# A batched matmul of 64x64 matrices: each load issued one store earlier in the DMA queue

## Chip, cores and metric

The kernel runs on one core of a Trainium2 chip. The metric is the device time of one execution in microseconds (us); lower is better.

## Reference

```python
def setup_inputs():
    return {
        "a": np.random.randn(1024, 64, 64).astype(np.float32),
        "b": np.random.randn(1024, 64, 64).astype(np.float32),
    }

def reference(a, b):
    return np.matmul(a, b).astype(np.float32)
```

There are 1024 independent products of two 64x64 matrices. Each of a, b and the output has 16.78 MB in float32.

## The kernel before

The 1024 matrices are cut in eight groups of 128 (`s` = 0 to 7, `n_s` = 8) for the loads, and in sixteen groups of 64 (`t` = 0 to 15, `n_t` = 16) for products and stores; group s feeds t = 2s and t = 2s + 1.

**Loads.** `load_a(s)` (line 79) and `load_pair(s)` (line 109) each issue four DMAs from POOL (GpSimd), of 32 partitions each. Each reads 512 KiB of float32 and writes 256 KB of bf16. "Tile a s" is what `load_a(s)` fills, "b pair s" what `load_pair(s)` fills. The first a tile is loaded otherwise, in float32 by four DMAs of the SP and ScalarE queues, into two buffers of the output pool (`load_first_a`). The pools `a_pool` and `b_pool` have three buffers each, so tile a s takes the buffer of a s-3 (a 1, 2 and 3 take the first three), and a load waits until VectorE has read what the buffer held.

**Turning.** VectorE transposes 32x32 blocks of a (`turn_a`, line 129) and b (`turn`, line 121), two instructions for each group s. `spread` (lines 142 and 149) copies the turned a of one t into a block diagonal tile `at_bd`, three quarters on VectorE and one on ScalarE; near both ends each engine does half. There are three such tiles (`N_BD`).

**Products and evacuation.** `multiply(t)` runs TensorE's matmuls (line 195) into PSUM, and ScalarE copies the results to an output tile `o_sb` (line 213, eight copies for each t). t = 14 is accumulated in another order, and t = 15 is cut in four parts whose copies ScalarE and VectorE share. Eight output tiles rotate.

**Stores.** `multiply` only notes a tile's stores in `held`; `store(t)` issues them. Each t has two halves of 512 KiB, both issued from POOL (line 222); only the last tile has four parts of 256 KiB on the SP and ScalarE queues.

**Order.** Each engine runs its instructions in the order in which the program writes them. Ahead of the loop come the first loads of a and b, groups 0 to 2. In the loop over t the order is `multiply(t)`, then the turns and spreads of later tiles, then `store(t)`. The table `BESIDE` (line 37) names the load that goes out with each store: half of its DMAs behind the first half of the store, half behind the second.

```python
        for i, piece in enumerate(held.pop(t)):
            piece()
            if load:
                load(s, range(2 * i, 2 * i + 2))
```

So POOL's queue of DMAs is: half store, two loads, half store, two loads, and so on, from store 0 to store 9; stores 10 to 14 have no loads beside them.

Of the kernel before, what the change touches and what calls it, by code (L numbers as in the profile page):

```python
# [12 lines left out]
def kernel(  # L13
# [21 lines left out]
    B_AHEAD = 3  # L35
    N_BD = 3
    BESIDE = {
        0: ("a", 3),
        1: ("p", 3),
        2: ("a", 4),  # L40
        3: ("p", 4),
        4: ("a", 5),
        5: ("p", 5),
        6: ("a", 6),
        7: ("p", 6),
        8: ("a", 7),
        9: ("p", 7),
    }
    LAST_QUEUE = {0: nc.sync, 2: nc.sync, 4: nc.scalar, 6: nc.sync}

# [28 lines left out]
    def load_a(s, hs=range(4)):  # L79
        if s not in a_tiles:  # L80
            a_tiles[s] = a_pool.tile([128, 4096], bf16, name="a_sb")
        for h in hs:
            nc.gpsimd.dma_start(out=a_tiles[s][32 * h : 32 * h + 32], in_=ap_v[s, h])  # L83

    def load_first_a():

        raw = [
            o_pool.tile([128, 8, 4, 64], fp32, name="o_sb")[:].rearrange(
                "p gh w n -> p (gh w n)"
            )  # L90
            for _ in range(2)
        ]
        parts = [raw[h % 2][:, 1024 * (h // 2) : 1024 * (h // 2) + 1024] for h in range(4)]
        for h in range(4):
            (nc.scalar if h % 2 else nc.sync).dma_start(out=parts[h], in_=a_v[0, h])
        a_tiles[0] = parts

    def turn_first_a(h):
        if h == 0:
            a_tiles["first"] = first.tile([128, 4, 1024], bf16, name="a_bf")  # L100
            at_tiles[0] = work.tile([128, 4, 8, 4, 4, 4], fp32, name="at_sb")
        rows = a_tiles["first"][:, h]
        (nc.scalar.copy if h else nc.vector.tensor_copy)(rows, a_tiles[0][h])  # L103
        nc.vector.transpose(  # L104
            at_tiles[0][:, h].rearrange("p g w mp vo -> p w vo g mp"),
            rows.bitcast(fp32).rearrange("p (vo w kp) -> p w vo kp", vo=4, w=4),
        )

    def load_pair(s, hs=range(4)):
        if 0 in hs:  # L110
            b_tiles[s] = b_pool.tile([128, 4096], bf16, name="b_sb")
        for h in hs:
            nc.gpsimd.dma_start(out=b_tiles[s][32 * h : 32 * h + 32], in_=bp_v[s, h])  # L113

    def turn(s, u):
        if u == 0:
            bbf_tiles[s] = work.tile([128, 32, 128], bf16, name="b_bf")
        rows = b_tiles[s][:].bitcast(fp32).rearrange("p (kp u np) -> p u np kp", kp=32, u=2)
        cols = bbf_tiles[s][:].rearrange("p g c -> p (g c)").bitcast(fp32)
        cols = cols.rearrange("p (g u np) -> p u np g", g=32, u=2)  # L120
        nc.vector.transpose(cols[:, u], rows[:, u])  # L121

    def turn_a(s, half):
        if half == 0:
            at_tiles[s] = work.tile([128, 32, 4, 4, 4], fp32, name="at_sb")
        rows = a_tiles[s][:].bitcast(fp32)
        rows = rows.rearrange("p (mp vo w kp) -> p mp vo w kp", mp=4, vo=4, w=4)
        cols = at_tiles[s][:].rearrange("p g w mp vo -> p mp vo w g")
        nc.vector.transpose(  # L129
            cols[:, 2 * half : 2 * half + 2].rearrange("p mp vo w g -> p (mp vo) w g"),  # L130
            rows[:, 2 * half : 2 * half + 2].rearrange("p mp vo w kp -> p (mp vo) w kp"),
        )
# [21 lines left out]
    def spread_all(t):  # L154
        on_act = (2, 3) if t < 2 or t >= n_t - 2 else (3,)
        spread(t, [h for h in range(4) if h not in on_act], nc.vector.tensor_copy)
        spread(t, on_act, nc.scalar.copy)

    def store(t):
        kind, s = BESIDE.get(t, ("", 0))  # L160
        load = {"a": load_a, "p": load_pair}.get(kind)
# [4 lines that stand above are left out]
# [52 lines left out]
    def multiply(t):  # L218
        o_sb = o_pool.tile([128, 8, 4, 64], fp32, name="o_sb")

        def put(lo, n):
            store_queue(t, lo).dma_start(  # L222
                out=o_v[t, :, lo : lo + n, :],
                in_=o_sb[:, lo : lo + n].rearrange("p gh w n -> p (gh w n)"),
            )

        act, dve = nc.scalar.copy, nc.vector.tensor_copy
        if t == n_t - 2:
            halves = [o_psum.tile([128, 4, 4, 64], fp32, name="o_ps") for _ in range(2)]
            for u in range(2):  # L230
                for half in range(2):
                    products(t, 8 * half, 8, halves[half], (u,))
                    if u == 1:
                        evacuate(t, 8 * half, 8, halves[half], o_sb, act)
        elif t == n_t - 1:
            for g0 in range(0, 16, 4):
                o_ps = t_psum.tile([128, 2, 4, 64], fp32, name="t_ps")
                products(t, g0, 4, o_ps)
                evacuate(t, g0, 4, o_ps, o_sb, dve if g0 % 8 else act)
        else:  # L240
            for g0 in (0, 8):
                o_ps = o_psum.tile([128, 4, 4, 64], fp32, name="o_ps")
                products(t, g0, 8, o_ps)
                evacuate(t, g0, 8, o_ps, o_sb, act)
        n = 2 if t == n_t - 1 else 4
        held[t] = [lambda lo=lo: put(lo, n) for lo in range(0, 8, n)]

    with tc.manual_schedule():
        load_first_a()
        nc.vector.memset(warm[:, 0:1], 0.0)  # L250
        nc.scalar.copy(warm[:, 1:2], warm[:, 0:1])  # L251
        nc.vector.memset(bd_tiles[0][:], 0.0)  # L252
        nc.gpsimd.memset(bd_tiles[1][:], 0.0)  # L253
        load_pair(0)
        load_a(1)
        load_pair(1)
        nc.gpsimd.memset(bd_tiles[2][:], 0.0)  # L257
        load_a(2)
        load_pair(2)
        for h in range(4):  # L260
            turn_first_a(h)
        spread_all(0)
        turn(0, 0)
        turn(0, 1)
        spread_all(1)
        turn_a(1, 0)
        turn_a(1, 1)
        spread_all(2)
        turn(1, 0)
        turn(1, 1)  # L270
        for t in range(n_t):
            s, half = t // 2, t % 2
            multiply(t)
            if t == 1:
                spread_all(3)
            elif half == 0 and s + 1 < n_s and t:
                turn_a(s + 1, 0)
                turn_a(s + 1, 1)
                spread_all(t + 2)
            elif half and s + 1 < n_s:  # L280
                if s + 1 == n_s - 1:
                    spread_all(t + 2)
                turn(s + 1, 0)
                turn(s + 1, 1)
                if s + 1 < n_s - 1:
                    spread_all(t + 2)
            store(t)
# [30 lines left out]
```

## Time and profile before

| What | Value |
|---|---|
| Median of 3 runs | 128.21 us (127.74 to 128.29) |
| Profiled execution | 128.62 us, of which its span is 126.8 us |
| Busy in the span | VectorE 102.9, ScalarE 96.0, POOL 64.9, TensorE 54.9 us |
| HBM | 33.55 MB read, 16.78 MB written, 397 GB/s over the span |
| POOL's DMA queue (q0) | 31.46 MB landed, 91.9% of the 16 DMA engines' span |
| Mean granted TensorE clock | 0.682 |

A page of the profile cuts the span in 40 slices of 3.17 us; a digit is the busy share of a slice in tenths. In a timeline, a row has its start, its length, the engine, the source line, the operation and, in brackets, the idle time before it with what ended it. In the windows, a row has the stretch, its length, the busy time of TensorE, its weight loads, VectorE, ScalarE and POOL with the instructions in parentheses, the granted clock, the DMA share and GB/s. The GB/s are those of what the DMAs wrote, so a load that turns float32 into bf16 counts half of what it reads. An issue row's length is POOL's time for writing the DMA's descriptors, not the transfer.

### The profile page before, as it was taken

To read this page: it belongs to the slowest core of one execution; us is meant where nothing else is said; L and a number is where in the kernel's file an instruction comes from. 1 tells how busy PE (TensorE), PEld (TensorE's weight loads), DVE (VectorE), ACT (ScalarE), POOL (GpSimd) and SP (SyncE) were. 2 spreads that over 40 slices of the span, in tenths; PEclk is the share of its full clock that TensorE was granted. 3 is DMA by queue.
4 is the path that set the end of the run, shared out by engine and by line. 5 is a ranking of instruction groups with operands and counts; after the bars stand their busy time and mean duration, and the time that the engine had idled before them with its cause. 6 is when DMAs were issued, how large, how long until landed. Compare 5 with 4: busy or idle time off the path is not lost.

```text
span 126.8 us, 2680 instructions
## 1 busy us (share of the span) xinstructions
PE 54.9 (43%) x1088; PEld 51.7 (41%) x1088; DVE 102.9 (81%) x93; ACT 96.0 (76%) x151; POOL 64.9 (51%) x96
## 2 busy tenths in 40 slices
PE   0000019028645485847352942047510777079400
PEld 0000019028645484847352932046510776079300
DVE  4956999999999999999969696896949789780810
ACT  2157920399999999999999889918898299999700
POOL 8962797428544655625544446474554464333100
PEclk9999999955586555555955599657755555555965
DMA  2999999999999999999999999999999999999992
GB/s 59 392 327 209 212 217 217 212 215 207 264 293 257 264 290 292 291 292 278 265 275 290 291 288 284 275 275 275 296 288 283 275 273 279 383 406 396 343 342 99
DMA packets 8875, 34.76 MB, mean 274 GB/s; under 512 B 1568, under 2 KB 2592, under 8 KB 6944
## 3 DMA queue, kind: packets, MB, share of 16 engines
q0 software_dynamic: 7200, 31.46, 91.9%
q1 hardware_dynamic: 1104, 1.84, 4.3%
q10 hardware_dynamic: 560, 1.31, 2.7%
q8 instruction: 8, 0.13, 0.4%
q14 instruction: 3, 0.02, 0.0%
HBM read 33.55 MB, written 16.78 MB: 397 GB/s over the span
## 4 chain that ended last, share of the span: by engine, by line
DMA 57%; DVE 15%; ACT 7%; issue 7%; PE 5%; POOL 3%; ACTq 1%; DVEq 0%; POOLq 0%
DMA a_sb<-in_a_dram 28%; DMA b_sb<-in_b_dram 15%; DMA out_dram<-o_sb 7%; DMA o_sb<-in_a_dram 7%; DVE at_sb L129 6%; ACT o_sb L213 4%; PE o_ps L195 3%; DVE b_bf L121 3%; POOL out_dram L222 3%; ACT at_bd L149 2%; DVE o_sb L213 2%; DVE at_bd L142 2%; PE t_ps L195 1%; DVE at_bd L149 1%; ACT a_bf L103 1%
## 5 line engine op out<-in xcount | busy, mean ns | idle before, releaser
L195 PE MATMUL o_ps<-b_bf,at_bd 128*128 128x64 bf16 (+1 forms) x1024 | 52.0, 232 | 63.7 <-ACT o_sb L213 35.7
L195 PEld LDWEIGHTS <-at_bd 128*128 128x128 bf16 (+1 forms) x1088 | 51.7, 127 | 66.8 <-issue 43.0
L213 ACT COPY o_sb<-o_ps 64x512 f32<-64x512 f32 x112 | 65.0, 580 | 7.7 <-PE o_ps L195 6.1
L222 POOL DMA_DIRECT2D out_dram<-o_sb x30 | 23.8, 792 | 31.1 <-DMA a_sb<-in_a_dram 8.4
L121 DVE STREAM_TRANSPOSE b_bf<-b_sb 128x1024 f32<-128x1024 f32 x16 | 34.3, 2195 | 4.9 <-DMA b_sb<-in_b_dram 4.7
L129 DVE STREAM_TRANSPOSE at_sb<-a_sb 128x1024 f32<-128x1024 f32 x14 | 26.2, 1948 | 3.8 <-issue 2.4
L149 DVE COPY at_bd<-at_sb 32x1024 f32<-32x1024 f32 x40 | 28.2, 705 | 1.1
L113 POOL DMA_DIRECT2D b_sb<-in_b_dram x32 | 17.7, 554 | 14.9 <-DMA b_sb<-in_b_dram 6.9
L149 ACT COPY at_bd<-at_sb 32x1024 f32<-32x1024 f32 x16 | 16.7, 1043 | 8.6 <-DVE at_sb L129 8.3
L83 POOL DMA_DIRECT2D a_sb<-in_a_dram x28 | 16.4, 590 | 6.3 <-DMA out_dram<-o_sb 4.7
L103 ACT CAST a_bf<-o_sb 128x1024 bf16<-128x1024 f32 x3 | 3.1, 1045 | 4.7 <-DMA o_sb<-in_a_dram 4.7
L213 DVE COPY o_sb<-t_ps 64x256 f32<-64x256 f32 x8 | 3.4, 422 | 3.9 <-PE t_ps L195 3.8
L104 DVE STREAM_TRANSPOSE at_sb<-a_bf 128x512 f32<-128x512 f32 x4 | 4.2, 1048 | 2.6 <-ACT a_bf L103 2.6
L142 ACT COPY at_bd<-at_sb 32x512 f32<-32x512 f32 x8 | 4.9, 615 | 0.2
L252 DVE MEMSET at_bd<- 128x4096 f32 x1 | 3.5, 3472 | 0.8 <-issue 0.8
L253 POOL MEMSET at_bd<- 128x4096 f32 x1 | 3.5, 3512 | 0.3 <-POOLq L302 0.3
L257 POOL MEMSET at_bd<- 128x4096 f32 x1 | 3.5, 3537 | 0.0
L142 DVE COPY at_bd<-at_sb 32x512 f32<-32x512 f32 x8 | 3.3, 414 | 0.2
L251 ACT ACT_TABLE_LOAD x1 | 1.3, 1283 | 2.3 <-issue 2.3
L195 PE MATMUL t_ps<-b_bf,at_bd 128*128 128x64 bf16 x64 | 3.0, 224 | 0.0
L213 ACT COPY o_sb<-t_ps 64x256 f32<-64x256 f32 x8 | 2.9, 367 | 0.1
L207 ACT COPY o_sb<-o_ps 128x1024 f32<-128x1024 f32 x2 | 1.9, 1015 | 0.1
(7 smaller groups left out, 1.4 us busy)
## 6 DMA issues: line engine op xcount, KB each, us to landing
out_dram<-o_sb POOLq DMA_DIRECT2D x30, 512.0 KB, 9.3
b_sb<-in_b_dram POOLq DMA_DIRECT2D x32, 256.0 KB, 9.5
a_sb<-in_a_dram POOLq DMA_DIRECT2D x28, 256.0 KB, 9.5
o_sb<-in_a_dram ACTq DMA_DIRECT2D x2, 512.0 KB, 7.4
o_sb<-in_a_dram SPq DMA_DIRECT2D x2, 512.0 KB, 5.8
out_dram<-o_sb SPq DMA_DIRECT2D x3, 256.0 KB, 5.4
out_dram<-o_sb ACTq DMA_DIRECT2D x1, 256.0 KB, 5.5
```

The costliest lines, as they stand in the source:

```text
L83: nc.gpsimd.dma_start(out=a_tiles[s][32 * h : 32 * h + 32], in_=ap_v[s, h])
L103: (nc.scalar.copy if h else nc.vector.tensor_copy)(rows, a_tiles[0][h])
L104: nc.vector.transpose(at_tiles[0][:, h].rearrange("p g w mp vo -> p w vo g mp"), rows.bitcast(fp32).rearrange("p (vo w kp) -> p w vo kp", ...
L113: nc.gpsimd.dma_start(out=b_tiles[s][32 * h : 32 * h + 32], in_=bp_v[s, h])
L121: nc.vector.transpose(cols[:, u], rows[:, u])
L129: nc.vector.transpose(cols[:, 2 * half : 2 * half + 2].rearrange("p mp vo w g -> p (mp vo) w g"), rows[:, 2 * half : 2 * half + 2].rearran ...
L142: copy(bd[rows, 8 * i : 8 * i + 8, :, h, :, :].rearrange("p g w mp vo -> p (g w) (mp vo)"), at_sb[block : block + 32, h].rearrange("p g w ...
L149: copy(bd[rows, :, :, h, :, :].rearrange("p g w mp vo -> p (g w) (mp vo)"), at_sb[rows, half].rearrange("p g w mp vo -> p (g w) (mp vo)"),)
L195: nc.tensor.matmul(place, at_bd[:, w, g, :, u], b_bf[:, g, 64 * u : 64 * u + 64], start=u == 0 and (first or not split), stop=u == 1 and ( ...
L213: copy(rows[64 * par : 64 * par + 64, :, :, wl, :], o_ps[64 * wl : 64 * wl + 64, :, par, :, :],)
L222: store_queue(t, lo).dma_start(out=o_v[t, :, lo : lo + n, :], in_=o_sb[:, lo : lo + n].rearrange("p gh w n -> p (gh w n)"),)
L252: nc.vector.memset(bd_tiles[0][:], 0.0)
```

## The change

Tile a 3 is loaded ahead of the loop, behind b pair 2 and so ahead of all stores. Every entry of `BESIDE` moves one store up: b pair 3 goes beside store 0, tile a 4 beside store 1, and so on to b pair 7 beside store 8. Nothing goes beside store 9. The loads, their sizes, their order among each other, the stores and the pools stay as they are.

```diff
     BESIDE = {
-        0: ("a", 3),
-        1: ("p", 3),
-        2: ("a", 4),
-        3: ("p", 4),
-        4: ("a", 5),
-        5: ("p", 5),
-        6: ("a", 6),
-        7: ("p", 6),
-        8: ("a", 7),
-        9: ("p", 7),
+        0: ("p", 3),
+        1: ("a", 4),
+        2: ("p", 4),
+        3: ("a", 5),
+        4: ("p", 5),
+        5: ("a", 6),
+        6: ("p", 6),
+        7: ("a", 7),
+        8: ("p", 7),
     }
...
         load_a(2)
         load_pair(2)
+        load_a(3)
         for h in range(4):
             turn_first_a(h)
```

## Prediction

> **What bounds the kernel now.** I read the page's slices first, to see which resource has no gaps.
>
> ```profile
> DVE  4956999999999999999969696896949789780810
> ACT  2157920399999999999999889918898299999700
> DMA  2999999999999999999999999999999999999992
> GB/s 59 392 327 209 212 217 217 212 215 207 264 293 257 264 290 292 291 292 278 265 275 290 291 288 284 275 275 275 296 288 283 275 273 279 383 406 396 343 342 99
> ```
>
> The DMA row is full from the second slice to the last but one. VectorE and ScalarE are full only in the first half. From about 62 us on VectorE has gaps, and the timeline of VectorE says what they wait for:
>
> ```profile
> 79.69 4.25 DVE L121 STREAM_TRANSPOSE b_bf<-b_sb 128x1024 f32<-128x1024 f32 x2 [1.48 <-DMA b_sb<-in_b_dram]
> 87.07 3.74 DVE L129 STREAM_TRANSPOSE at_sb<-a_sb 128x1024 f32<-128x1024 f32 x2 [1.22 <-DMA a_sb<-in_a_dram]
> 94.58 4.24 DVE L121 STREAM_TRANSPOSE b_bf<-b_sb 128x1024 f32<-128x1024 f32 x2 [1.60 <-DMA b_sb<-in_b_dram]
> 109.37 4.31 DVE L121 STREAM_TRANSPOSE b_bf<-b_sb 128x1024 f32<-128x1024 f32 x2 [0.67 <-DMA b_sb<-in_b_dram]
> ```
>
> It waits for loads that are still in the queue. The timeline of POOL, which issues all loads but the first and all stores but the last tile's, shows the queue's pace:
>
> ```profile
> 78.99 0.79 POOL L222 DMA_DIRECT2D out_dram<-o_sb  x1 [0.68 <-DMA b_sb<-in_b_dram]
> 80.08 0.51 POOL L113 DMA_DIRECT2D b_sb<-in_b_dram  x1 [0.30 <-issue]
> 81.15 0.50 POOL L113 DMA_DIRECT2D b_sb<-in_b_dram  x1 [0.56 <-DMA out_dram<-o_sb]
> 82.67 0.79 POOL L222 DMA_DIRECT2D out_dram<-o_sb  x1 [1.02 <-DMA a_sb<-in_a_dram]
> 83.51 1.02 POOL L113 DMA_DIRECT2D b_sb<-in_b_dram  x1
> 84.86 0.50 POOL L113 DMA_DIRECT2D b_sb<-in_b_dram  x1 [0.33 <-DMA out_dram<-o_sb]
> 86.37 0.79 POOL L222 DMA_DIRECT2D out_dram<-o_sb  x1 [1.01 <-DMA a_sb<-in_a_dram]
> ```
>
> Each issue waits for an older transfer to land. One round, from 78.99 to 86.37, is two half stores and four loads. Four such rounds, from the store at 71.54 to the one at 101.20, take 29.66 us: 7.42 us each, 1.24 us per transfer. Each transfer has 512 KiB on its HBM side (a load arrives as 256 KB of bf16), so 6 x 524,288 bytes in 7.42 us are 424 GB/s at the HBM. A transfer lands 9.3 to 9.5 us after its issue (the table of issues), so some seven to eight are always queued. Last, the windows, a row per stage (the last two numbers are the DMA share and GB/s landed):
>
> ```profile
> 12.00:27.00 15.00, 3.73 (x64) 3.62 (x65) 14.59 (x17) 7.35 (x13) 9.46 (x12) 0.95 1.04 214
> 62.00:107.00 45.00, 22.05 (x435) 20.72 (x432) 36.81 (x32) 37.21 (x60) 24.20 (x36) 0.63 1.03 281
> 109.00:112.00 3.00, 0.33 (x13) 0.36 (x15) 2.63 (x2) 2.92 (x6) 1.51 (x2) 0.50 1.03 411
> 112.00:115.00 3.00, 2.97 (x109) 2.81 (x106) 1.68 (x1) 2.83 (x4) 0.75 (x1) 0.50 1.02 400
> 115.00:117.00 2.00, 2.00 (x52) 1.94 (x47) 0.00 (x0) 2.00 (x3) 0.75 (x1) 0.50 1.06 404
> 117.00:119.00 2.00, 1.60 (x41) 1.48 (x38) 1.45 (x4) 1.92 (x7) 0.75 (x1) 0.80 0.96 342
> 119.00:121.00 2.00, 0.00 (x0) 0.00 (x0) 1.93 (x5) 0.67 (x2) 0.00 (x0) 1.00 1.00 348
> 121.00:124.00 3.00, 0.00 (x0) 0.00 (x0) 0.00 (x0) 0.00 (x0) 0.00 (x0) 0.53 1.01 340
> 124.00:126.80 2.80, 0.00 (x0) 0.00 (x0) 0.00 (x0) 0.00 (x0) 0.00 (x0) 0.50 0.18 62
> ```
>
> Loads alone land at 214 GB/s, which is 428 read. Loads and stores together land at 281; at the HBM that is the 424 worked out above. Stores alone start at 411 and 400, and fall to 340 to 348 from 117 us. All of that is at a DMA share of about 1. Although the last copy of VectorE ends at 121.0 us and the last store is issued then, the DMA engines are still full to 124: what ends last is not the compute but the sum of all bytes.
>
> **The change, part by part.** No transfer is added or removed; a fixed number of bytes goes through a resource that is always busy. So the time can move only through idle DMA time, or through the pace.
>
> *Tile a 3 ahead of store 0.* The four loads join the queue right after b pair 2, whose last issue is at 24.31 us. In the trace before, POOL then sat 2.92 us until ScalarE had finished tile 0 (27.85 us); but with 9.5 us of transfers queued the DMA share stayed 1.03. So filling that gap is worth 0. Four issues of 0.59 us (2.4 us) and their waits for older transfers now stand on POOL ahead of store 0, which goes out five turns of the queue after 24.31: at 24.31 + 5 x 1.24 = 30.5 us, 2.7 later. Nobody waits for store 0 soon: its output buffer is used again eight tiles later.
>
> *Every later load one store earlier, b pair 7 beside store 8.* Each load passes one store, two transfers: 2 x 1.24 = 2.47 us earlier. It needs its buffer earlier, and the loads behind it on POOL would wait too. The reader to be done for a 5 (beside store 3) is the turn of a 2, which ends at 36.4 us, against an issue of that store at 48.81; for a 6, the turn of a 3 ends at 49.0, against 64.14; for b pair 7, the turn of pair 4 ends at 69.2, against 86.37. Twelve us or more of margin each: 0. If that cover were gone, POOL would stand still, yet only a wait longer than the 9.5 us queue would reach the DMA engines.
>
> *VectorE's stalls.* From 62 us on its timeline has seven before turns; they add up to 0.98 + 1.21 + 1.48 + 1.22 + 1.60 + 1.21 + 0.67 = 8.4 us. With loads 2.47 us earlier the first of them vanish until VectorE is 2.47 us ahead; then it waits for loads again. So the last evacuation ends near 118.5 us instead of 121.0. This does not end the kernel: at 118.5 the queue holds two half stores more than it would have. Worth 0 at the end.
>
> *The pace.* This is what is left. The last load lands about 2.47 us earlier, and two half stores (1.05 MB) that ran between loads now run in the stretch of stores alone, which grows from ten halves and the last tile to twelve and the last tile. In the mix they cost 2.47 us. The bounds are the fastest and the slowest pace of that stretch: at 411 GB/s 2.55 us (+0.08), at 340 GB/s 3.08 us (+0.61). Neither row tells which end is extended, so I take the mean pace of the whole stretch: (3 x 411 + 3 x 400 + 2 x 404 + 2 x 342 + 2 x 348 + 3 x 340) / 15 = 376 GB/s, 2.79 us, **+0.32 us**. A bound below zero is kept by the second rival.
>
> A rule beside that row: the Trainium skill's page "HBM Reference", section Specifications (TRN2), gives about 358 GB/s as a core's share of its HBM, and about 425 for a core that streams alone. The 424 to 428 of this trace agrees with its second figure, but the 340 of the tail lies below both; by 358 the two half stores would take 2.93 us, an estimate of +0.46, which would leave the forecast where it is.
>
> **Sum.** The profiled execution took 128.62 us (span 126.8 plus 1.82 around it), 0.41 above the median of 128.21; the change of +0.32 gives 128.94 on its own scale, and 128.53 on the median's. I forecast 128.5 us. A run of this kernel tells about 0.5% (0.64 us) from no change.
>
> **Rivals.**
>
> *Slower: the slow pace starts earlier and takes in more.* If the 340 GB/s come from how long stores have run alone (they set in 7.6 us after the last load has landed at 109.37), or from the last tile's stores on the SP and ScalarE queues mixing with POOL's (first issue at 118.18), the slow stretch starts 2.47 us earlier and 1.05 MB more falls into it. At 340 that is +0.61. If the mixing of three queues also spreads over more of POOL's stores, another half store goes at 1.54 instead of 1.30 us: +0.24, so 0.85 and 129.1 us. It decides where the windows after fall under 350 GB/s by 115 us instead of 117. For it: the fall lasts to the end once begun. Against it: it begins together with VectorE's last copies at 117.51, which keep their length.
>
> *Faster: a thin queue is what slows the tail.* POOL waits 2.48, 1.61 and 2.50 us for evacuations in the tail, and before the store at 116.14 only three halves are queued (those issued in the 9.3 us before, at 109.29, 110.51 and 112.88). If short queues slow the engines, the two extra halves keep 404 GB/s to the end of POOL's stores. The bytes after 117 us are about 2.6 MB; 1.5 MB without the last tile's, at 404 instead of 342 are 3.7 instead of 4.4 us: -0.7; with the last tile's as well, -1.2. Less the +0.08 above, 127.1 to 127.6; I take 127.4. Against it: the DMA share is 0.96 to 1.01 there, so packets are slow, not missing.
>
> *The loads do not come earlier,* since a buffer is held longer than I read: 128.2 us.
>
> **Numbers.** Forecast (+0.08 to +0.61) 0.50, of which 0.05 passes the bound of slower; slower rival 0.25, of which 0.05 stays within; faster rival 0.15, of which 0.03 stays within; no advance 0.05; what I do not see 0.05 (0.03 slower, 0.02 faster). So faster 0.14, same 0.58, slower 0.28. The forecast's own range, with the 0.2 us by which runs differ, is 128.1 to 129.0; out to the faster and slower rivals' points it is 127.4 to 129.2.
>
> **What would show it.** Right: the DMA row full to the last but one slice; loads alone to about 37 us, four transfers longer; VectorE's wait before the last b pair's turn ending near 106.9; its last copy near 118.5; the last store issued there, landing no earlier than now. Wrong: a DMA share clearly under 1 anywhere between 5 and 122 us; windows of stores alone that keep 400 to the end (faster) or fall to 340 before 115 us (slower); POOL's load issues waiting for VectorE.

## The result, and the profile after

The changed kernel takes 129.05 us (median of 6 runs, 128.59 to 129.25) against 128.08 us (6 runs, 127.74 to 128.29) beside it: 0.97 us more, a ratio of 1.0074 (95% interval 1.0048 to 1.0099). It is slower by 0.7%, somewhat over the 0.5% that the prediction set as its bound. Some executions of these kernels fall into a slower state, some 3 to 4 us longer; the times and ratios of this document leave those out.

Its profiled execution took 129.25 us with a span of 127.4 us. That is 0.63 us above the profiled execution of before, not 0.97: the profile of before lay 0.54 us above its median, that of after 0.20. So the two traces show some two thirds of the difference.

The rows of the page after, in 40 slices of 3.19 us:

```profile
DMA  3999999999999999999999999999999999999992
GB/s 73 399 323 206 219 211 214 208 219 208 216 199 270 300 295 289 287 264 266 280 297 296 278 286 271 270 282 298 293 275 278 282 270 383 405 378 350 349 338 90
```

The DMA engines are full throughout, as before. Loads alone (about 210 GB/s landed) go on to slice 12, 38 us, instead of slice 10, since tile a 3 is now among them. At the other end five slices of stores alone have become six, and three of them are near 345 where there were two.

VectorE's timeline after; each row has the start, the length and, in brackets, the wait before it:

```profile
69.88 3.74 DVE L128 STREAM_TRANSPOSE at_sb<-a_sb 128x1024 f32<-128x1024 f32 x2 [0.28 <-DMA a_sb<-in_a_dram]
77.25 4.23 DVE L120 STREAM_TRANSPOSE b_bf<-b_sb 128x1024 f32<-128x1024 f32 x2 [1.44 <-DMA b_sb<-in_b_dram]
106.92 4.27 DVE L120 STREAM_TRANSPOSE b_bf<-b_sb 128x1024 f32<-128x1024 f32 x2 [0.47 <-DMA b_sb<-in_b_dram]
114.16 3.48 DVE L212 COPY o_sb<-t_ps 64x256 f32<-64x256 f32 x8 [2.97 <-PE t_ps L194]
```

The last b pair's turn starts at 106.92 instead of 109.37, 2.45 us earlier, and the last copy ends at 117.64 instead of 121.0. The compute is done 3.4 us sooner and the kernel ends later. The windows of the tail after (stretch, length, busy times of TensorE, weight loads, VectorE, ScalarE and POOL, granted clock, DMA share, GB/s) show what ends last:

```profile
109.00:112.00 3.00, 2.78 (x93) 2.67 (x95) 2.19 (x2) 2.94 (x4) 2.25 (x3) 0.50 1.04 407
112.00:115.00 3.00, 3.00 (x107) 2.89 (x103) 0.82 (x2) 2.94 (x6) 1.19 (x2) 0.86 1.01 371
115.00:117.00 2.00, 0.06 (x2) 0.00 (x0) 1.92 (x6) 1.93 (x6) 0.32 (x1) 1.00 1.04 358
117.00:119.00 2.00, 0.00 (x0) 0.00 (x0) 0.63 (x2) 0.19 (x1) 0.00 (x0) 1.00 1.00 340
119.00:121.00 2.00, 0.00 (x0) 0.00 (x0) 0.00 (x0) 0.00 (x0) 0.00 (x0) 0.67 1.00 351
121.00:124.00 3.00, 0.00 (x0) 0.00 (x0) 0.00 (x0) 0.00 (x0) 0.00 (x0) 0.50 1.00 338
124.00:127.40 3.40, 0.00 (x0) 0.00 (x0) 0.00 (x0) 0.00 (x0) 0.00 (x0) 0.50 0.29 102
```

In the same stretches the kernel before had 411, 400, 404, 342, 348 and 340 GB/s. From 109 us on both have 5.8 MB left to store, so up to there neither is ahead. At 124 us the kernel before has 62 x 2.8 = 174 KB left, this one 102 x 3.4 = 347 KB, which at 340 GB/s is 0.5 us. The fall from 400 comes in the window 112 to 115 instead of at 117.

### The profile page after: what moved, and what is told of

Read it like the earlier page. It is cut to its first block, busy times and chain, and to the rows that moved or that the text cites. A ratio compares the mean times of both kernels' runs of the same rounds, so it can differ in the third digit from the quotient of the medians.

```text
span 127.4 us, 2680 instructions
## 1 busy us (share of the span) xinstructions
PE 52.9 (42%) x1088; PEld 49.7 (39%) x1088; DVE 102.5 (80%) x93; ACT 96.0 (75%) x151; POOL 66.1 (52%) x96
## 3 DMA queue, kind: packets, MB, share of 16 engines
q10 hardware_dynamic: 560, 1.31, 2.7%
## 4 chain that ended last, share of the span: by engine, by line
DMA 38%; ACT 28%; DVE 9%; POOL 7%; issue 5%; PE 4%; DVEq 0%; POOLq 0%; ACTq 0%
DMA a_sb<-in_a_dram 30%; ACT o_sb L212 22%; DMA out_dram<-o_sb 7%; DVE at_sb L128 6%; ACT at_bd L148 6%; PE o_ps L194 3%; POOL at_bd L252 3%; DVE o_sb L212 2%; POOL b_sb L112 2%; DVE at_bd L141 1%; POOL out_dram L221 1%; POOL a_sb L82 1%; PE t_ps L194 1%; DVEq L313 0%; DVEq L128 0%
## 5 line engine op out<-in xcount | busy, mean ns | idle before, releaser
L194 PE MATMUL o_ps<-b_bf,at_bd 128*128 128x64 bf16 (+1 forms) x1024 | 50.9, 230 | 62.2 <-ACT o_sb L212 30.5
L194 PEld LDWEIGHTS <-at_bd 128*128 128x128 bf16 (+1 forms) x1088 | 49.7, 125 | 65.3 <-issue 48.9
L221 POOL DMA_DIRECT2D out_dram<-o_sb x30 | 24.4, 814 | 25.4 <-ACT o_sb L212 6.4
L112 POOL DMA_DIRECT2D b_sb<-in_b_dram x32 | 18.6, 582 | 13.3 <-DMA b_sb<-in_b_dram 6.3
L194 PE MATMUL t_ps<-b_bf,at_bd 128*128 128x64 bf16 x64 | 2.0, 193 | 0.0
```

What stands on the lines that cost most here:

```text
L194: nc.tensor.matmul(place, at_bd[:, w, g, :, u], b_bf[:, g, 64 * u : 64 * u + 64], start=u == 0 and (first or not split), stop=u == 1 and ( ...
L221: store_queue(t, lo).dma_start(out=o_v[t, :, lo : lo + n, :], in_=o_sb[:, lo : lo + n].rearrange("p gh w n -> p (gh w n)"),)
```

## The experiments

The theory, L: stores that run with no load between them slow down some 7 us after the last load, so what counts is how many stores come after the last load. The rivals: O, the four loads ahead of store 0 cost the start; C, the pace falls because of what the engines do for the last tiles.

**The first half alone.** In the kernel before:

```diff
-        0: ("a", 3),
...
         load_pair(2)
+        load_a(3)
```

> The first half of the change alone: tile a 3 ahead of all stores, nothing beside store 0, the other loads where they were, so the last b pair stays beside store 9 and ten half stores and the last tile run after the loads, as before. Theory L (the length of the run of stores alone sets the time, since its pace falls after some 7 to 9 us): as before, ratio 0.998 to 1.002. Rival O (four loads ahead of store 0 cost it: stores late, buffers late): as the whole change, ratio 1.006 or more. Rival C (the pace falls because of what the last tiles' copies do, wherever they fall in the tail): as before, ratio about 1.000.

Measured: 129.1 us, ratio 1.0074 (1.0054 to 1.0095). As it stands this speaks for O and against L and C, which both expected no change. Its trace has two things that the whole change does not have. VectorE's wait for the last b pair ends 1.26 us later than before (110.63), and the tail's windows show the DMA engines running dry:

```profile
115.00:117.00 2.00, 1.99 (x84) 1.95 (x84) 0.00 (x0) 1.98 (x3) 0.00 (x0) 0.82 1.04 393
117.00:119.00 2.00, 1.46 (x51) 1.34 (x46) 1.39 (x4) 1.96 (x6) 1.51 (x2) 1.00 0.87 326
```

With nothing beside store 0, three half stores stand in a row in the queue at its beginning; that this is what delays the loads was not tried. So this run did not separate the two, and a cleaner one was needed.

**The last pair kept.** The whole change, with only the last b pair left where it was. This is the cleaner one: its start is exactly that of the change.

```diff
-        8: ("p", 7),
+        9: ("p", 7),
```

> The whole change, but the last b pair stays beside store 9 (nothing beside store 8): ten half stores and the last tile after the loads, as before; the start and all other loads as after the change. Theory L (the length of the run of stores alone): as before, ratio 0.998 to 1.003. Rival O (the four loads ahead of store 0, which the first experiment shared): as the whole change, 1.006 to 1.009.

Measured: 128.68 us (12 runs), ratio 1.0028 (0.9999 to 1.0058). O had expected 1.006 or more, so it falls for the change as a whole; a cost of the start of up to 0.7 us stays possible by this interval. Two half stores moved behind the last load are the difference between 1.0028 and 1.0074, some 0.6 us; the two intervals together leave about 0.1 to 1.1 us.

The tail of this run shows that the number of stores after the last load is not all that counts. The last b pair's turn starts at 109.18, as before the change (109.37), and ten half stores follow, but the pace falls sooner. First this run, then the kernel before:

```profile
113.00:115.00 2.00, 1.84 (x70) 1.72 (x67) 0.51 (x1) 0.33 (x1) 0.00 (x0) 0.50 1.04 381
115.00:117.00 2.00, 2.00 (x66) 1.94 (x61) 0.21 (x1) 1.99 (x4) 0.86 (x2) 0.76 1.01 369
```

```profile
113.00:115.00 2.00, 1.97 (x76) 1.83 (x72) 0.68 (x1) 1.86 (x3) 0.63 (x1) 0.50 1.01 397
115.00:117.00 2.00, 2.00 (x52) 1.94 (x47) 0.00 (x0) 2.00 (x3) 0.75 (x1) 0.50 1.06 404
```

Here nothing goes beside store 8, so three half stores stand in a row ahead of the last pair, as they do at store 0 in the run of the first half. Stores without loads may cost there too; that was not tried.

**The last pair alone.** In the kernel before, b pair 7 goes beside store 8 together with a 7 (`store` then takes a list of loads):

```diff
-        8: ("a", 7),
-        9: ("p", 7),
+        8: (("a", 7), ("p", 7)),
```

> The last part of the change alone: b pair 7 goes beside store 8 together with a 7, all other loads where they were. Twelve half stores and the last tile then run after the loads, as after the change. L: as the whole change, ratio 1.005 to 1.010 (129.0 us). O: as before, 1.000. C: the copies of the last tiles come earlier by up to 2.47 us here too, so 1.005 to 1.010 as well.

Measured: 129.4 us, ratio 1.0095 (1.0070 to 1.0120). It is the number that L expected, but not for L's reason alone. The two kinds of loads alternate, so a 7's second half lands later (its last load is issued at 94.34, against 92.28 before, and loads take 9.5 us to land); VectorE waits for it, and the tail's stores come too late to keep the DMA engines busy:

```profile
104.16 3.73 DVE L128 STREAM_TRANSPOSE at_sb<-a_sb 128x1024 f32<-128x1024 f32 x2 [3.65 <-issue]
```

```profile
117.00:119.00 2.00, 2.00 (x63) 1.94 (x58) 0.02 (x1) 2.00 (x3) 0.75 (x1) 0.70 0.83 295
119.00:121.00 2.00, 0.87 (x30) 0.75 (x26) 1.93 (x5) 1.93 (x6) 0.75 (x1) 1.00 0.80 268
```

Shares of 0.83 and 0.80 over four us are some 0.7 us of empty DMA engines. That is a second cost, opposite to the first: a queue that runs dry. This run cannot tell how much of its loss is which.

**One store further.** The whole change, and b pair 7 beside store 7:

```diff
-        7: ("a", 7),
-        8: ("p", 7),
+        7: (("a", 7), ("p", 7)),
```

> The whole change, and b pair 7 one store earlier still, beside store 7 with a 7: fourteen half stores and the last tile after the loads. L: each two half stores that join the run of stores alone go at 340 to 350 GB/s instead of 424, +0.57 to +0.9 each, so ratio 1.012 to 1.016 (129.6 to 130.1 us). C: the compute of the last tile can move ahead by less, since VectorE has fewer waits left to lose, so the slow pace starts hardly earlier: 1.007 to 1.010.

Measured: 130.05 us, ratio 1.0139 (1.0114 to 1.0164), as L expected, and beyond what C allowed. Here too a 7 and b pair 7 alternate, and VectorE waits 3.79 us before it turns a 7, but the tail is not dry anywhere:

```profile
109.00:111.00 2.00, 0.00 (x0) 0.00 (x0) 1.97 (x2) 1.95 (x4) 0.99 (x2) 0.50 1.00 393
111.00:113.00 2.00, 1.17 (x37) 1.08 (x39) 2.00 (x2) 1.94 (x5) 0.52 (x1) 0.50 1.04 365
115.00:117.00 2.00, 2.00 (x60) 1.94 (x56) 0.00 (x0) 2.00 (x3) 0.69 (x1) 0.63 1.02 338
117.00:119.00 2.00, 1.02 (x35) 0.89 (x31) 1.81 (x5) 1.93 (x6) 0.81 (x2) 1.00 1.00 328
```

The pace is down to 365 by 113 us and 338 by 117, while VectorE's copies of the last tile begin at 117.12 and the last tile's stores on the SP queue at 118.35. So neither the last copies nor the mixing of three queues sets off the fall. Ten, twelve and fourteen half stores after the last load give ratios of 1, 1.0074 and 1.0139 in the kernel before, the change and this run. The other runs are not on that line: 1.0074 and 1.0028 with ten, 1.0095 with twelve. So the number alone does not set the time.

**The other way.** The kernel before, with the last b pair one store later:

```diff
-        9: ("p", 7),
+        10: ("p", 7),
```

> The other way: the kernel before with the last b pair one store later, beside store 10: eight half stores and the last tile after the loads. L alone: 0.5 to 0.9 us faster, ratio 0.993 to 0.996. Theory T (two-sided: the queue of before holds just enough stores to cover the compute after the last load, some 11.7 us): the DMA share falls to 0.3 to 0.7 for 2 to 3 us near 118 us, the last copies of VectorE end near 123.5, and the time is 1 to 2 us longer, ratio 1.007 to 1.016.

Measured: 129.76 us (median of five runs, 129.17 to 131.11), ratio 1.0122 (1.0062 to 1.0181). Fewer stores at the end are slower too, as theory T expected. Only the time is read from this run; that the queue runs dry in it, as T has it, is not shown.

**The kernel before once more**, for a second trace.

> The kernel before once more, for a second profile: the profiled execution of the first was 0.4 to 0.5 us above the median. Theory S (a slow start of that one execution, its first transfers later and its engines further apart): about 128.1 us, the first load landed 0.2 us earlier and one stall of 0.4 us fewer around the first store, the tail as in the first profile. Rival: the tail differs between executions, and the first profile showed a tail that is slower than usual.

Measured: 129.0 us in its one execution. Theory S fell: the loads of this execution come later than in the first profile, not earlier. The first b pair's turn starts 0.69 us later (14.99 against 14.30), the last one's 1.45 us later (109.37 in the first profile):

```profile
110.82 4.31 DVE L121 STREAM_TRANSPOSE b_bf<-b_sb 128x1024 f32<-128x1024 f32 x2 [0.68 <-DMA b_sb<-in_b_dram]
```

The tail differs as well. This execution's windows have a dry stretch that the first profile of before has hardly (0.96 at the same place):

```profile
117.00:119.00 2.00, 1.87 (x64) 1.75 (x60) 1.00 (x3) 1.98 (x5) 1.25 (x2) 1.00 0.65 244
```

So both marks of the run of the first half, a last pair at 110.63 and a dry tail, occur in the kernel before itself, at the same time of 129 us, and can't be put down to that run's edit. What sets that run apart is that all six of its times lie at 128.99 to 129.31, and the eleven of the kernel before beside it at 127.83 to 128.81.

Together with the run of the last pair one store later, this suggests that the order of before stands near a balance: its stores after the last load last about as long as the compute after it, and an execution whose loads come 1.45 us late already runs dry.

**The DMA queue by itself**, in both orders. These two kernels leave out all compute; their stores send what a memset left:

```diff
-            piece()
+            nc.gpsimd.dma_start(out=o_v[t, :, lo : lo + 4, :], in_=tiles[t % 4][...])  # shortened
```

> Only POOL's DMAs in the order of before, nothing computed (the stores send what a memset left, the first a tile is not loaded, the last tile goes from POOL too). Theory L (the DMA queue alone makes the difference): after the last load twelve half stores at first at 1.27 to 1.30 us each, then 1.5 to 1.7. 60 loads and 20 stores between them at 1.24 us. Rival C (the tail is slow by what the engines do): 1.24 to 1.30 us to the end.

> The same with the order of the change: fourteen half stores after the last load. L: 0.5 to 1.0 us longer than in the order of before. C: within 0.2 us of it.

Measured: 123.95 us (123.67 to 123.95) and 124.65 us (124.53 to 124.77), 0.70 us between them with no compute at all. The windows of the order of before (here the columns are VectorE, POOL, clock, DMA share, GB/s, and so in all that follow):

```profile
107.00:109.00 2.00, 0.00 (x0) 1.38 (x3) 1.00 1.04 410
109.00:111.00 2.00, 0.00 (x0) 1.26 (x2) 1.00 1.03 373
111.00:113.00 2.00, 0.00 (x0) 0.00 (x0) 1.00 1.00 348
```

and of the order of the change:

```profile
105.00:107.00 2.00, 0.00 (x0) 1.86 (x3) 1.00 1.02 399
107.00:109.00 2.00, 0.00 (x0) 1.28 (x2) 1.00 1.03 354
109.00:111.00 2.00, 0.00 (x0) 0.98 (x2) 1.00 1.01 358
```

The fall comes some 2 us earlier, and the pace after it is about the same (328 to 358). The last load is issued 2.87 us earlier in the order of the change, so the four loads ahead of store 0 cost the queue nothing up to there:

```profile
95.05 0.50 POOL L72 DMA_DIRECT2D b_sb<-in_b_dram  x1 [0.86 <-DMA out_dram<-o_sb]
92.18 0.50 POOL L71 DMA_DIRECT2D b_sb<-in_b_dram  x1 [0.82 <-DMA out_dram<-o_sb]
```

So the order of the transfers alone makes a difference of 0.70 us, in the run of stores alone, and C is out as the cause of the fall.

**Stores alone**, first as the kernel has them, then with the 4 KB of a partition written in one piece, last in three shapes. The edit of the second:

```diff
-    o_v = out.rearrange("(t gh x) (mo w) n -> t (x mo) gh (w n)", gh=8, x=8, w=4)
+    o_v = out.rearrange("(t c x) (mo w) n -> t c (x mo) (w n)", c=2, x=32, w=16)
```

> Only the stores, same shapes, order and queues, from four tiles that a memset fills: no loads, no compute, the output holds ones. L: a pace of 400 to 410 GB/s for the first 7 to 9 us, then 340 to 350 to the end: 16.78 MB in 3.3 MB / 405 + 13.5 MB / 345 = 47 us of transfers. C: 400 to 410 to the end but for the last tile's 1 KB packets: 41 to 42 us of transfers.

> Stores alone again, but each partition writes 4 KB in one piece (the output's rows are taken in another order, all stores from POOL). Theory W (writes alone have a lower ceiling): 320 to 345 GB/s as in the stores alone before. Rival P (it is the pattern of 1 KB pieces, with all engines on the same step of it): 400 GB/s or more.

> Stores alone, all from POOL, in three stretches: six tiles as halves of 128 partitions with 4 KB in pieces of 1 KB (as the kernel has them), five tiles as halves of 64 partitions with 8 KB, five tiles as one store of 1 MB. Theory L as first put (a run of stores alone starts at 400 and tires after 7 to 9 us): the first stretch starts at 400 GB/s. Rival P (the pace is that of 16 engines all on 1 KB pieces; the kernel's tail starts faster because its engines come spread out from the loads): 320 to 345 from the start, and the other stretches differ from the first by over 5%.

Measured: 62.78, 53.7 and 66.98 us, one execution each. The windows of the first, of the second, and of the third (halves of 128 partitions, halves of 64 partitions, whole tiles):

```profile
17.00:27.00 10.00, 0.00 (x0) 4.32 (x7) 1.00 1.01 329
37.00:47.00 10.00, 0.00 (x0) 4.51 (x6) 1.00 1.01 326
```

```profile
13.00:23.00 10.00, 0.00 (x0) 3.72 (x7) 1.00 1.02 390
33.00:43.00 10.00, 0.00 (x0) 2.91 (x6) 1.00 1.02 390
```

```profile
8.00:24.00 16.00, 0.00 (x0) 8.87 (x14) 1.00 1.01 322
28.00:36.00 8.00, 0.00 (x0) 2.59 (x4) 1.00 0.99 285
48.00:57.00 9.00, 0.00 (x0) 0.00 (x0) 1.00 1.00 337
```

Stores as the kernel has them go at 322 to 329 GB/s steadily when they run alone; the two other shapes, in 1 KB pieces as well, go at 285 and 337. None of the three runs starts with 7 us at 400 (from 6 to 11 us the first and the third have 274 to 348): that part of L, as first put, is wrong, and the transfers of the first run take some 53 us, more than both theories gave. The slow pace is the normal one of such stores alone. That the 400 GB/s at the start of the kernel's tail are a carry-over from the stretch in which loads ran between them is the reading left, but not shown. Pieces of 4 KB keep 390, just under the 400 that rival P expected, and the time bears it out: 53.7 against 62.78 us.

**The order of the change with 4 KB pieces**, DMAs only:

> Only POOL's DMAs in the order of the change, as in the earlier run (124.65 us), but each partition's 4 KB of a store go to the output in one piece (the rows land in another order; nothing computed, the first a tile not loaded). If the fall of the pace in the run of stores alone comes from the pieces of 1 KB: no fall below 380 GB/s in the tail, 0.7 to 1.5 us faster (123.2 to 124.0). If any long run of stores tires the queue: the fall comes 7 us after the last load here too, 124.4 to 124.9.

```profile
107.00:109.00 2.00, 0.00 (x0) 0.94 (x2) 1.00 1.04 424
113.00:115.00 2.00, 0.00 (x0) 0.00 (x0) 1.00 1.04 426
117.00:119.00 2.00, 0.00 (x0) 0.00 (x0) 1.00 0.47 191
119.00:121.00 2.00, 0.00 (x0) 0.00 (x0) 1.00 0.00 0
```

The pace does not fall at all, and the transfers are over at 118 us, some 2 us before those with 1 KB pieces. So by the transfers that the profile shows, the fall is tied to how the stores are written. The edit changes two things at once: a partition writes one piece of 4 KB instead of four of 1 KB, and it has no more pieces that lie 128 KB apart. Which of the two counts was not tried. And the time does not bear it out: the run took 125.37 us (125.13 to 125.51), longer, not shorter, and more than either expectation allowed. Its span ends at 123.6 us, some 5 us after the last transfer that the profile shows (some 2 us with 1 KB pieces), and what fills these us was not found.

None of the orders tried beats the kernel before.

## Why the prediction was right and where it failed

- *What bounds the kernel.* Right: the DMA share stays at 1.00 to 1.04 in the tail, and compute that ended 3.4 us sooner bought nothing.
- *Tile a 3 ahead of store 0, worth 0.* Store 0 went out at 30.17 us (30.5 expected), and the last b pair came 2.45 us earlier, almost the full 2.47, so in these traces the start cost nothing up to there. The run with the last pair kept has the same start and a ratio of 1.0028, whose interval goes from just below 1 to 1.0058; by the times, a cost of up to 0.7 us stays possible.
- *Later loads 2.47 us earlier, no buffer waits.* Right: 2.45 us for the last. By the profile one load issue of POOL (55.44 us) waited for VectorE, 0.43 us, with the queue full; the prediction had named such waits as a sign of being wrong.
- *VectorE's stalls.* Right in kind: from 62 us on the waits before its turns add up to 0.28 + 1.44 + 1.35 + 1.31 + 1.34 + 0.47 = 6.2 us instead of 8.4. The last copy ended at 117.64, not 118.5.
- *The pace.* Here the forecast failed. The mechanism was right, two half stores more in the run of stores alone, but the term was mis-sized: 376 GB/s, the mean over that run, gave +0.32 us. In these traces the stretch at 400 ended sooner and the run grew at its slow end, not by its mean. The prediction wrote that neither row told which end is extended; the price of the slow end, +0.61, was its upper bound. The DMA queue alone measured +0.70, the last pair's place in the full kernel about 0.6, and the whole change +0.97, which is above that bound.
- *The slower rival* (+0.61 to 0.85, 129.1 us, chance 0.25) comes nearest: the slow stretch starts earlier and takes in more. Its own test, windows under 350 GB/s by 115 us, was not met: they fall to 371 from 112 us and 358 from 115, and under 350 only from 117. Its first trigger, a fixed time after the last load, fits the queue alone; in the kernels the fall starts 4 to 8 us after the wait for the last pair ends (7.6 before, some 6 after, some 4 with the last pair kept). Its second trigger, the last tile's stores on three queues, is refuted as the start of the fall by the run with the pair at store 7 and by the queue alone, where POOL issues all stores.
- *The faster rival*, that a thin queue slows the engines, is refuted: after the change five half stores are queued before the store at 113.65, where three were before the one at 116.14, and the pace falls sooner. What a thin queue does is run dry, with shares of 0.65 to 0.87.
- *A rule beside the row.* "HBM Reference" of the Trainium skill, Specifications (TRN2), has about 358 GB/s for a core's share of its HBM. The 326 to 329 of stores alone are below it and the 390 to 426 of 4 KB pieces above it, so that figure is not what holds the tail. That 4 KB pieces run at 424 by their packets agrees with its 425 for a core alone.
- The forecast of 128.5 us was 0.55 too low. The time lies just outside the forecast's own range of 128.1 to 129.0 and inside the wide one of 127.4 to 129.2. That is partly luck: as a difference, +0.97 is three times the forecast and more than even the slower rival's +0.85, but the kernel before measured 128.08 here instead of 128.21. The likeliest class, no change, was missed, if narrowly.

Three things stay open: why stores of 1 KB pieces keep 400 GB/s for 4 to 8 us after the last load, the part of the whole change between 0.70 and 0.97 us, and why the first half alone costs as much as the whole.

## What to carry to other kernels

In a kernel like this one, whose DMA engines are always full, bringing loads forward gains nothing by itself; it only changes which transfers run together. Price what is pushed to the end at the pace of the very end, not at a mean. And look at both sides: here both fewer and more stores after the last load were slower. More of them run at their own slow pace; with fewer the queue probably runs dry before the compute ends.

## What the hardware showed that was not expected

Stores whose rows reach the output in pieces of 1 KB run at 322 to 329 GB/s when nothing else runs, and at full pace (424 GB/s for both kinds together, at the HBM) when loads are mixed in. Splitting the same store by 64 partitions makes it worse (285), a store of 1 MB little better (337), pieces of 4 KB in one stretch much better (390 alone, and 416 to 426 by its packets behind a mixed stretch, though that run's time was no shorter).
